# Raw float32 for the shared expert and router, a new plan of expert units, and gates between head pairs

## The chip, the cores and the metric

One core of a Trainium2 chip runs the kernel. The metric is the time of one execution in device microseconds. A matrix engine (TensorE, PE in the rows; PEld are its weight loads), VectorE (DVE), ScalarE (ACT), GpSimd (POOL) and SyncE (SP, which here only issues DMAs) have their own instruction streams and wait for one another by semaphores.

## The reference, cut to what matters

Two transformer blocks on 256 tokens of width 1024, all in float32.

The first block projects the normed input `h` to eight parts, runs a windowed attention (8 heads, with a bias table and a mask) and a grouped attention (8 query heads, 2 key heads, with norms and rotary positions), and merges them under two gates:

```python
proj = h @ w_in
qa, ka, va, qb, kb, vb, ga, gb = split(proj)
ya = neighbourhood_attention(qa, ka, va, rpb)
yb = gqa_attention(axial_rope(rmsnorm(qb)), axial_rope(rmsnorm(kb)), vb)
x = x + (sigmoid(ga) * (ya @ w_proj_a) + sigmoid(gb) * (yb @ w_proj_b)) @ w_out
```

A large layer of retrieved experts follows, and then the second block: a modulated mixer of two recurrences, and a mixture of 64 experts of which each token takes 8, with one shared expert:

```python
scores = sigmoid(h @ w_router)                  # 256 tokens x 64 experts
sel = scores + router_bias                      # 4 of 8 groups, then the 8 best experts
gates = chosen scores, normed, times 2.5
routed = sum over experts of (silu(h @ w_gate[e]) * (h @ w_up[e]) * gate[:, e]) @ w_down[e]
shared = (silu(h @ ws_gate) * (h @ ws_up)) @ ws_down
```

## The kernel before, in words

**Split products.** Most weights come as blocks of 128 x 1024 float32 into a raw tile; `split` (lines 66, 67) has ACT copy it to a high half `whi` in the faster matmul format float32r and DVE (or POOL, where asked) subtract to get the low half `wlo`. `mm3` (lines 80 to 82) multiplies high by high, high by low and low by high. `wide_load` makes a loader over a ring of raw tiles, and another over pairs of halves; with `whole` it returns the raw tile unsplit, which is multiplied in float32.

**First block** (`block1_mix`). The normed input is turned to `hT` (high and low). `stationary` and `moving` multiply it by the blocks of `w_in`, with 4 raw tiles and 2 pairs of halves. The program's order is: queries and keys of the windowed attention, its values, the four head pairs of the windowed attention, the projections of the grouped one, their norms and rotation on DVE (lines 270 to 309), its four head pairs, and the 16 gate blocks (lines 314 to 319), the first eight of which have POOL subtract. The mask is added to the bias table by one POOL instruction over 3072 elements (line 246). Only the first DMAs have an order written out by hand; for the rest a planner orders each engine's instructions, so gates and projections may run under an attention.

**Mixture** (`moe`). From the last steps of the mixer on, SP, PE, DVE and ACT keep the order of the program. The shared expert's four gate/up blocks and the router's block are split; its two down blocks are raw (`shared_up`, line 1587; the router, lines 1603 to 1605; `shared_down`). Then comes the choice of experts, a chain of small DVE steps (lines 1637 to 1774), which sorts the experts by their count of tokens into ranks and gives SP the list `lst` of their addresses. The first `STATIC` experts are put at the front whatever their count, so that their weights can be asked for before the list (`pre`).

The ranks are put into units of 128 columns of tokens: ranks below `WIDE` have all 128, below `MID` 96, below `LIGHT` 64, below `REST` 32. `mixture` joins them: a 96 with a 32, two of 64, four of 32 (or two of 32 and one of 64), and orders the kinds by a place between 0 and 1. Columns that a rank doesn't have are run by extra branches, which are taken only if a count is larger. An expert's weights are four gate/up blocks and two down blocks, and TensorE works on narrow columns of several experts side by side.

`run` goes through the units. In the turn of unit u TensorE does the gate/up matmuls (line 1559), between them the gather of a later group of two units (line 1743) and the turn of the unit before (line 1570), then the combining of unit u - 2 into the four sums in PSUM (line 1840) and the down matmuls of unit u - 1 (line 1578). `ahead` asks for weights on SP in the order of their use; a ring of 25 tiles takes them: raw tiles of the stage (4), of a pool opened at the start of `moe` (4) and of a later one (3), two tiles of the modulation, and the tiles of the shared weights' halves (12).

Of the kernel before, what the change touches and what calls it, by code (L numbers as in the profile page):

```python
# [19 lines left out]
P = 128  # L20
# [33 lines left out]
def uid(e, s):  # L54
    e.n += 1
    return f"{s}_{e.n}"
# [86 lines left out]
def block1_mix(e, a, x, begin):  # L143
# [22 lines left out]
    qkT = pool.tile([P, 8, T], F32, name="qkT")  # L166

    def stationary(blk, out, eng=None):
# [10 lines left out]
    def moving(blks, width, per):  # L179

        pt = [ps.tile([P, 512], F32, tag="mm", name=uid(e, "pmv"), bufs=e.mm_bufs) for _ in range(2)]
        for i, b in enumerate(blks):
            wh, wl = load_w(e, a["w_in_b"][b])
# [56 lines left out]
    for b in (0, 4, 1, 5):  # L240
# [5 lines left out]
    nc.gpsimd.tensor_tensor(bias.rearrange("p a b c -> p (a b) c"), bias.rearrange("p a b c -> p (a b) c"),  # L246
                            mask[:, None, :].to_broadcast([P, 48, 64]), op=OP.add)
# [9 lines left out]
    bv = bias.rearrange("p h v c -> p h (v c)")  # L257
# [22 lines left out]
    for tt, qk in enumerate(qks):  # L280
# [28 lines left out]
        nc.vector.tensor_copy(kT[:, :, tt * P:(tt + 1) * P], p[:, :2])  # L309
    for pair in range(4):  # L310
# [4 lines left out]
    sg = keep.tile([P, 16, T], F32, name="sg")  # L315
    for b in range(16):
        p = ps.tile([P, 512], F32, tag="mm", name=uid(e, "pg"), bufs=e.mm_bufs)
        stationary(8 + b, p[:, :T], nc.gpsimd if b < 8 else None)
        nc.scalar.activation(sg[:, b], p[:, :T], AF.Copy)
# [1076 lines left out]
STATIC = 2  # L1396
WIDE = 7
MID = 16
LIGHT = 30
REST = 50  # L1400
AHEAD = 8
RAW0 = 4
RAW1 = 3
# [41 lines left out]
def mixture():  # L1445

    few = iter(range(LIGHT, REST))
    kinds = [[shared((r, P)) for r in range(STATIC, WIDE)],
             [shared((r, 96), (next(few), 32)) for r in range(WIDE, MID)],
             [shared((r, 64), (r + 1, 64)) for r in range(MID, LIGHT, 2)]]  # L1450
    few = list(few)
    kinds.append([shared(*((r, 32) for r in few[i:i + 4])) for i in (0, 4)] + [shared((few[8], 32), (few[9], 32), (few[10], 64))])
    at = lambda k, j, n: j / (n - 1) if k == 0 else (j + 0.5) / n
    order = sorted((at(k, j, len(us)), k, u) for k, us in enumerate(kinds) for j, u in enumerate(us))
    return [u for _, _, u in order]
# [12 lines left out]
def moe(e, a, x, m, late, out):  # L1468
# [6 lines left out]
    load = wide_load(e, [(early, RAW0), (e.stage, e.raw_bufs)], [(early, 4), (e.stage, e.w_bufs)])  # L1475
# [28 lines left out]
    wg = [load(a["ws_gu"][b]) for b in range(2)]  # L1504
# [8 lines left out]
    wg.append(load(a["ws_gu"][2]))  # L1513
    wr = load(a["w_router"], eng=nc.gpsimd)
# [8 lines left out]
    hT = pool.tile([P, 2, NC8, T], F32R, tag="ehT", name="ehT")  # L1523
    hT = [hT[:, i] for i in range(2)]
# [4 lines left out]
    lows = [turned(e, h[0], 4 * n, 0, *hT) for n in range(2)]  # L1529
    add_to(1, m.po[1], 1, mod[2])  # L1530
    square(1, 1)
    for f in lows:
        f()
# [13 lines left out]
    def gu_block(pg, xh, xl, b, w):  # L1547
        for k in range(2):
            c = 2 * b + k
            s = slice(k * 512, (k + 1) * 512)  # L1550
            for j, (l, r) in enumerate(((xh, 0), (xh, 1), (xl, 0))):
                nc.tensor.matmul(pg, l[:, c], w[r][:, s], start=c == 0 and j == 0, stop=c == NC8 - 1 and j == 2)
# [34 lines left out]
    def shared_up(tt, b):  # L1587
        gu_block(pg[tt], hT[0][:, :, tts[tt]], hT[1][:, :, tts[tt]], b, wg[b])
# [5 lines left out]
    wg.append(load(a["ws_gu"][3], eng=nc.gpsimd))  # L1594
    lows = [turned(e, h[1], 4 * n, 1, *hT) for n in range(2)]
    for f in lows:
        f()
# [4 lines left out]
    wh, wl = (w.rearrange("p (c n) -> p c n", c=NC8) for w in wr)  # L1602
# [17 lines left out]
    wd = [load(a["ws_dn"][k], True) for k in range(2)]  # L1620
    units = [[(r, 0, P, 0)] for r in range(STATIC)] + mixture()
# [5 lines left out]

    load.raw[:0] = [(early, 4, t) for _ in range(4) for t in ("whi", "wlo")]
    load.raw[:0] = [(e.stage, e.w_bufs, t) for _ in range(e.w_bufs) for t in ("whi", "wlo")]
# [174 lines left out]
    def run(units, acc=(), new=None, ready=()):  # L1804
# [39 lines left out]
        ahead(1)  # L1844
# [63 lines left out]
        v = pool.tile([P, NC8, 2, T], F32R, tag="ehT", name=uid(e, "v")).bitcast(F32)  # L1908
        for tt in range(2):
            half = [slice(n * 512, (n + 1) * 512) for n in range(2)]  # L1910
            vs = [v[:, 2 * tt + n].rearrange("p a b -> p (a b)") for n in range(2)]
# [24 lines left out]
    if e.overflow:  # L1936
        with tc.If(nc.values_load(moreu[:, 5:6], min_val=0, max_val=T) > 0):
# [5 lines left out]
            with tc.If(v[2] > 0):  # L1943
                run([shared((r, 64), (r + 1, 64), base=64) for r in range(MID, LIGHT, 2)] + [shared((MID, P), base=P)])
            with tc.If(v[1] > 0):
                run([shared((r, P), base=96) for r in range(WIDE, MID)]
                    + [shared(*((r, 32) for r in range(WIDE, WIDE + 4)), base=224)])
# [97 lines left out]
```

## Time and profile before

| | |
|---|---|
| median of 3 runs | 1759.52 us (1758.49 to 1759.73) |
| the profiled execution | 1763.74 us, its span 1761.9 us |
| busy share: PE, DVE, ACT, POOL | 94%, 64%, 43%, 11% |
| DMA | 390.91 MB, mean 222 GB/s |
| mean granted clock of TensorE | 0.981 of full speed |

All rows are of the profiled execution, with times from its span's start. A share of busy time is a mean over stages that have different limits; windows and waits tell them apart. The first block runs until about 176 us, the layer of retrieved experts until about 1050, the mixer until about 1285, and the mixture from there to the end.

### The profile page before, as it was taken

What the parts mean: (1) busy time and instruction counts of PE and PEld (TensorE: products, weight loads), DVE (VectorE), ACT (ScalarE), POOL (GpSimd) and SP (SyncE); (2) the same over time, 40 slices, a digit from 0 to 9 for tenths busy, and PEclk for the clock granted to TensorE, in tenths of its full rate; (3) what the DMA queues carried; (4) which work ended last, traced back from release to release, by engine and by line L of the source; (5) the groups of instructions that cost most, each with busy time, mean ns of one, the idle gap of its engine ahead of it and who ended that gap; (6) DMA issues with size and microseconds to landing.
All of it is one profiled execution on the core that took longest, in us unless ns stands there. A gap on an engine that the chain in (4) does not pass through costs nothing.

```text
span 1761.9 us, 29814 instructions
## 1 busy us (share of the span) xinstructions
PE 1660.2 (94%) x11419; PEld 1307.8 (74%) x11419; DVE 1133.1 (64%) x2214; ACT 750.5 (43%) x1224; POOL 190.5 (11%) x95
## 2 busy tenths in 40 slices
PE   6989999899989999999999997987989999999996
PEld 6778888899989999777788776977875444444443
DVE  5675779995989999877777767688673111111112
ACT  3547544444544444444444455655552222222222
POOL 1030001222111222000000003023020000000000
PEclk9999999999999999999999999998999999999999
DMA  6423654556545555587888754532067799999993
GB/s 232 131 84 109 214 163 158 160 158 192 155 126 162 169 171 177 172 283 265 308 283 295 261 165 144 181 118 72 13 238 282 266 392 409 409 402 409 409 409 132
DMA packets 108118, 390.91 MB, mean 222 GB/s; under 512 B 12656, under 2 KB 12944, under 8 KB 107840
## 3 DMA queue, kind: packets, MB, share of 16 engines
q1 hardware_dynamic: 106128, 384.58, 62.7%
q0 software_dynamic: 976, 2.82, 0.5%
q8 instruction: 91, 1.49, 0.3%
q10 hardware_dynamic: 864, 1.53, 0.3%
q14 instruction: 59, 0.48, 0.1%
HBM read 386.79 MB, written 2.10 MB: 221 GB/s over the span
## 4 chain that ended last, share of the span: by engine, by line
PE 67%; DVE 18%; DMA 7%; issue 4%; ACT 3%; POOL 0%; SPq 0%; DVEq 0%; ACTq 0%
PE pgu L1559 11%; PE acc L686 10%; PE py L1578 6%; PE pu L80 5%; PE pu L81 5%; PE pu L82 5%; DVE wlo L67 5%; DMA raw<-in_w_ada 4%; PE pga L1743 3%; PE py L1840 3%; PE pg L632 2%; ACT whi L66 2%; PE pmv L81 1%; PE pmv L82 1%; PE pmv L80 1%
## 5 line engine op out<-in xcount | busy, mean ns | idle before, releaser
L66 ACT ACTIVATE whi<-raw 128x1024 fp32r<-128x1024 f32 x366 | 384.5, 1054 | 307.7 <-PE pu L81 136.7
L67 DVE TENSOR_TENSOR wlo<-raw,whi 128x1024 fp32r<-128x1024 f32 x310 | 383.4, 1239 | 83.1 <-ACT whi L66 82.0
L82 PE MATMUL pu<-pxT,wlo 128*128 128x256 f32 x1024 | 289.7, 283 | 9.2 <-DVE wlo L67 6.7
L80 PE MATMUL pu<-pxT,whi 128*128 128x256 f32 x1024 | 292.3, 285 | 0.8 <-ACT whi L66 0.8
L81 PE MATMUL pu<-pxT,whi 128*128 128x256 f32 x1024 | 288.9, 282 | 0.0
L686 PE MATMUL acc<-whi,hh 128*128 128x512 f32 x1008 | 280.7, 396 | 8.5 <-ACT hh L66 5.8
L686 PEld LDWEIGHTS acc<-whi,hh 128*128 128x128 f32 x1008 | 189.1, 189 | 53.9 <-ACT hh L66 6.8
L67 POOL TENSOR_TENSOR wlo<-raw,whi 128x1024 fp32r<-128x1024 f32 x56 | 149.6, 2675 | 661.9 <-ACT whi L66 607.2
L82 PEld LDWEIGHTS pu<-pxT,wlo 128*128 128x128 f32 x1024 | 195.3, 191 | 11.1 <-DVE wlo L67 8.1
L80 PEld LDWEIGHTS pu<-pxT,whi 128*128 128x128 f32 x1024 | 195.4, 191 | 1.0 <-ACT whi L66 1.0
L81 PEld LDWEIGHTS pu<-pxT,whi 128*128 128x128 f32 x1024 | 195.4, 191 | 0.0
L1559 PE MATMUL pgu<-raw,xg 128*32 128x512 f32 (+2 forms) x1012 | 193.8, 597 | 0.0
L686 PE MATMUL acc<-wlo,hh 128*128 128x512 f32 x504 | 157.5, 393 | 2.8 <-DVE wlo L67 2.8
L66 ACT ACTIVATE hh<-H 128x256 fp32r<-128x256 f32 x126 | 52.6, 417 | 174.6 <-PE acc L686 169.9
L1559 PEld LDWEIGHTS pgu<-raw,xg 128*32 128x32 f32 (+2 forms) x1012 | 55.6, 124 | 92.3 <-issue 82.1
L686 PEld LDWEIGHTS acc<-wlo,hh 128*128 128x128 f32 x504 | 95.0, 189 | 24.3 <-DVE wlo L67 4.2
L67 DVE TENSOR_TENSOR yl<-py,yh 128x512 fp32r<-128x512 f32 x52 | 36.0, 691 | 110.7 <-ACT yh L66 110.6
L1578 PE MATMUL py<-raw,th 128*32 128x512 f32 (+2 forms) x504 | 99.9, 599 | 0.5 <-ACT th L1572 0.5
L1564 DVE SCALAR_TENSOR_TENSOR hh<-hh,sv,pgu 128x256 f32<-128x256 f32 x26 | 12.4, 478 | 124.5 <-ACT hh L1563 124.5
L771 DVE SCALAR_TENSOR_TENSOR ada<-raw,cs,ada 128x1024 f32<-128x1024 f32 x48 | 61.5, 1282 | 40.6 <-DMA raw<-in_w_ada 40.6
L1746 ACT ACTIVATE xg<-pga 128x256 f32<-128x256 f32 x104 | 40.0, 384 | 111.6 <-PE pga L1743 107.6
L1743 PEld LDWEIGHTS pga<-S,hs 128*128 128x128 f32 x416 | 54.5, 188 | 36.8 <-issue 36.1
(567 smaller groups left out, 2919.5 us busy)
## 6 DMA issues: line engine op xcount, KB each, us to landing
raw<-in_w_gu SPq DMA_DIRECT2D x186, 512.0 KB, 9.6
raw<-in_peer_u SPq DMA_DIRECT2D x128, 512.0 KB, 3.6
raw<-in_peer_v SPq DMA_DIRECT2D x128, 512.0 KB, 4.5
raw<-in_w_dn SPq DMA_DIRECT2D x90, 512.0 KB, 10.1
raw<-in_w_ada SPq DMA_DIRECT2D x48, 512.0 KB, 4.8
raw<-in_w_in_a SPq DMA_DIRECT2D x24, 512.0 KB, 3.6
raw<-in_w2a SPq DMA_DIRECT2D x17, 512.0 KB, 4.4
raw<-in_w_out SPq DMA_DIRECT2D x16, 512.0 KB, 3.6
```

What stands on the lines that cost most here:

```text
L66: e.nc.scalar.activation(hi, src, AF.Copy)
L67: (eng or e.nc.vector).tensor_sub(lo, src, hi.bitcast(F32))
L80: nc.tensor.matmul(out, lh, rh, start=first, stop=False)
L81: nc.tensor.matmul(out, lh, rl, start=False, stop=False)
L82: nc.tensor.matmul(out, ll, rh, start=False, stop=last)
L686: nc.tensor.matmul(acc[tt][n], h[l][:, s], w[r][:, n * 512:(n + 1) * 512], start=j == order[0] and i == 0, stop=j == order[-1] and i == 2)
L771: nc.vector.scalar_tensor_tensor(mod[n], w, cs[:, c:c + 1], mod[n], op0=OP.mult, op1=OP.add)
L1559: nc.tensor.matmul(pg[t], xx[:, c, t], ws[i][:, k * 512:(k + 1) * 512], start=c == 0, stop=c == NC8 - 1)
L1578: nc.tensor.matmul(py[q][t], th[:, k, t], w[i][:, q * 512:(q + 1) * 512], start=k == 0, stop=last and k == 1)
L1743: nc.tensor.matmul(p[:, :n].rearrange("p u n -> p (u n)"), hs[i][:, tt, q * P:(q + 1) * P], S[:, tt, :n].rearrange("p u n -> p (u n)"), st ...
L1746: nc.scalar.activation(xg[:, q, :n], p[:, :n], AF.Copy)
L1840: nc.tensor.matmul(acc[tt][n], St[:, tt * P:(tt + 1) * P], y[:, n * 512:(n + 1) * 512], start=first and v == 0 and w == 0, stop=v == len(u ...
```

## The change: what it does

1. `moe`: the shared expert and the router multiply raw float32 tiles, in one matmul each; the turned input is kept once, not as two halves. The pool at the start has 12 raw tiles in place of 4 and 8 halves, the later one 5 in place of 3.
2. Three fixed experts in place of two; `WIDE` 6 for 7, `MID` 14 for 16. The list has 25 units, not 26: 3 fixed, then 3 of one expert, 8 of 96 + 32, 8 of 64 + 64 and 3 of four times 32, one of which is the first after the fixed.
3. `ahead` counts blocks of both kinds, up to 27, the size of the ring now.
4. `block1_mix`: `w_in` uses 4 pairs of halves; the windowed attention stands behind the grouped projections and their rotation; two gates stand behind each head pair of both attentions, all split by ACT and DVE; the mask is added by DVE, two heads at a time.

```diff
     def stationary(blk, out, eng=None):
-        wh, wl = load_w(e, a["w_in_a"][blk], eng=eng)
+        wh, wl = load(a["w_in_a"][blk], eng=eng)
...
-    nc.gpsimd.tensor_tensor(bias.rearrange("p a b c -> p (a b) c"), bias.rearrange("p a b c -> p (a b) c"),
-                            mask[:, None, :].to_broadcast([P, 48, 64]), op=OP.add)
...
-    for pair in range(4):
-        attention(pair, lambda q: qkT[:, q], lambda q: qkT[:, 4 + q],
-                  lambda q, kc: va[:, kc, q * P:(q + 1) * P], lambda h: bv[:, h], yT[0])
...
+    def gate(b):
+        p = ps.tile([P, 512], F32, tag="mm", name=uid(e, "pg"), bufs=e.mm_bufs)
+        stationary(8 + b, p[:, :T])
+        nc.scalar.activation(sg[:, b], p[:, :T], AF.Copy)
...
+    def masked(h):
+        if h % 2 == 0:
+            v = bias[:, h:h + 2].rearrange("p a b c -> p (a b) c")
+            nc.vector.tensor_tensor(v, v, mask[:, None, :].to_broadcast([P, 12, 64]), op=OP.add)
+        return bv[:, h]
+
+    for pair in range(4):
+        attention(pair, lambda q: qkT[:, q], lambda q: qkT[:, 4 + q],
+                  lambda q, kc: va[:, kc, q * P:(q + 1) * P], masked, yT[0])
+        for b in (2 * pair, 2 * pair + 1):
+            gate(b)
     for pair in range(4):
         attention(pair, lambda q: qT[:, q], lambda q: kT[:, q // 2],
                   lambda q, kc: vb[:, kc, q // 2].rearrange("p a b -> p (a b)"), None, yT[1])
-    for b in range(16):
...
+        for b in (8 + 2 * pair, 9 + 2 * pair):
+            gate(b)
...
-STATIC = 2
-WIDE = 7
-MID = 16
+STATIC = 3
+WIDE = 6
+MID = 14
...
-AHEAD = 8
-RAW0 = 4
-RAW1 = 3
+LEAD = 27
+RAW0 = 12
+RAW1 = 5
...
+    kinds = [[shared((r, P)) for r in range(STATIC, WIDE)],
+             [shared((WIDE + i, 96), (few[i], 32)) for i in range(n)],
+             [shared((r, 64), (r + 1, 64)) for r in range(MID, LIGHT, 2)],
+             [shared(*((r, 32) for r in few[i:i + 4])) for i in range(n, len(few), 4)]]
+
+    at = ([0.15, 0.33, 0.84], None, None, [0.0, 0.3, 0.8])
...
-            for j, (l, r) in enumerate(((xh, 0), (xh, 1), (xl, 0))):
-                nc.tensor.matmul(pg, l[:, c], w[r][:, s], start=c == 0 and j == 0, stop=c == NC8 - 1 and j == 2)
+            nc.tensor.matmul(pg, x[:, c], w[:, k * 512:(k + 1) * 512], start=c == 0, stop=c == NC8 - 1)
...
-        mm3(e, p[:, :T], wh[:, c], wl[:, c], hT[0][:, c], hT[1][:, c], c == 0, c == NC8 - 1)
+        nc.tensor.matmul(p[:, :T], wr[:, c], hT[:, c], start=c == 0, stop=c == NC8 - 1)
...
-        def ahead(n=AHEAD):
-            while len(ready) < len(order) and sum(1 - o[0] for o in order[taken[0]:len(ready)]) < n:
+        def ahead(n=LEAD):
+            while len(ready) < min(len(order), taken[0] + n):
```

The extra branches are cut anew to the same effect, and the loads of the shared weights and the router lose their splits.

## Rows read from the trace of the kernel before

**Rows 1.** The page's first part: busy us (share of the span) xinstructions of each engine.
```profile
PE 1660.2 (94%) x11419; PEld 1307.8 (74%) x11419; DVE 1133.1 (64%) x2214; ACT 750.5 (43%) x1224; POOL 190.5 (11%) x95
```

**Rows 2.** Windows by stage: stretch, length, busy us (xinstructions) per engine, clock, DMA, GB/s.
```profile
15.00:30.00 15.00, 11.55 (x79) 11.34 (x79) 8.62 (x7) 3.22 (x4) 6.78 (x1) 0.89 0.51 168
...
90.00:130.00 40.00, 31.58 (x213) 29.02 (x211) 30.77 (x58) 19.42 (x39) 17.30 (x7) 0.91 0.26 79
130.00:176.00 46.00, 45.55 (x316) 40.35 (x315) 24.78 (x48) 32.32 (x64) 0.00 (x0) 1.00 0.37 115
1285.00:1312.00 27.00, 23.36 (x105) 17.84 (x103) 21.47 (x32) 12.63 (x21) 4.10 (x5) 1.00 0.89 332
...
1385.50:1708.40 322.90, 322.70 (x2188) 145.66 (x2188) 52.64 (x120) 69.94 (x165) 0.00 (x0) 1.00 1.01 398
```

**Rows 3.** Chain of waits in the experts' stretch: start us, us, what.
```profile
1380.27 1.88 PE py L1840 x8
...
1385.59 3.57 PE pgu L1559 x32
...
1708.42 1.88 PE py L1840 x8
...
1734.17 1.89 PE py L1840 x8
...
1742.55 3.45 PE py L1578 x8
```

**Rows 4.** Windows, and SP's waits (total us, times, longest), experts' stretch.
```profile
1365.00:1425.00 60.00, 59.96 (x375) 28.50 (x377) 10.23 (x23) 13.56 (x32) 0.00 (x0) 1.00 0.83 290
1425.00:1720.00 295.00, 294.82 (x2006) 132.65 (x2002) 47.40 (x107) 63.64 (x150) 0.00 (x0) 1.00 1.03 408
...
1730.00:1746.00 16.00, 15.39 (x71) 7.30 (x69) 2.07 (x4) 2.95 (x6) 0.00 (x0) 1.00 0.02 6
...
SPq L1417 <- PE pgu L1559: 31.6, 37, 2.7
SPq L1811 <- DVE lst L1765: 14.4, 1, 14.4
```

**Rows 5.** Chain of waits, then groups by line (busy, mean ns, idle before), shared expert.
```profile
1323.13 5.81 PE pgu L1552 x24
...
1348.27 3.43 PE pgu L1559 x8
...
L81 PE MATMUL po<-wlo,mhT 128*128 128x512 f32 x29 | 11.4, 393 | 1.1 <-DVE wlo L67 1.1
L1552 PE MATMUL pgu<-whi,ehT 128*128 128x512 f32 x32 | 10.8, 404 | 0.7 <-DVE ehT L1344 0.7
...
L1341 PE MATMUL ptr<-ident,eh 128*128 128x128 f32 x16 | 2.3, 277 | 1.6 <-DVE eh L1496 0.8 <-PE po L82 0.8
```

**Rows 6.** Timeline, start of the first block: start us, us, engine, line, operation.
```profile
16.90 6.78 POOL L246 TENSOR_TENSOR bias<-bias,mask 128x3072 f32<-128x3072 f32 x1 [15.58 <-DMA mask<-in_na_mask]
...
19.38 5.38 DVE L67 TENSOR_TENSOR wlo<-raw,whi 128x1024 fp32r<-128x1024 f32 x1 [0.55 <-ACT whi L66]
...
24.82 0.38 PE L82 MATMUL pqk<-hT,wlo 128*128 128x256 f32 x1 [3.45 <-DVE wlo L67]
25.02 1.21 DVE L67 TENSOR_TENSOR wlo<-raw,whi 128x1024 fp32r<-128x1024 f32 x1
```

**Rows 7.** Timeline of DVE, and POOL's splits grouped by line, first block.
```profile
107.01 2.88 DVE L283 TENSOR_TENSOR qk<-qk,gq 128x512 f32<-128x512 f32 x1
...
111.16 0.68 DVE L299 TENSOR_TENSOR qk<-qk,ro 128x512 f32<-128x512 f32 x1
...
L67 POOL TENSOR_TENSOR wlo<-raw,whi 128x1024 fp32r<-128x1024 f32 x8 | 19.7, 2458 | 85.9 <-ACT whi L66 83.9 <-PE pg L82 2.0
```

**Rows 8.** Chain of waits, second attention, first pair.
```profile
120.25 1.07 PE pS L204 x8
...
127.51 1.79 PE pY L235 x8
```

More of the change, by code (lines that the diff above doesn't have):

```diff
@@ L1445, in mixture @@
 def mixture():
-    few = iter(range(LIGHT, REST))
+    few = list(range(LIGHT, REST))
+    n = MID - WIDE
     kinds = [[shared((r, P)) for r in range(STATIC, WIDE)],
[L1449 to L1454, printed above, removed]
+             [shared((WIDE + i, 96), (few[i], 32)) for i in range(n)],
+             [shared((r, 64), (r + 1, 64)) for r in range(MID, LIGHT, 2)],
+             [shared(*((r, 32) for r in few[i:i + 4])) for i in range(n, len(few), 4)]]
+    at = ([0.15, 0.33, 0.84], None, None, [0.0, 0.3, 0.8])
+    order = sorted((at[k][j] if at[k] else (j + 0.5) / len(us), k, u) for k, us in enumerate(kinds) for j, u in enumerate(us))
     return [u for _, _, u in order]
@@ L1474, in moe @@
     mod = m.mod
-    load = wide_load(e, [(early, RAW0), (e.stage, e.raw_bufs)], [(early, 4), (e.stage, e.w_bufs)])
+    load = wide_load(e, [(early, RAW0), (e.stage, e.raw_bufs)], [])
     def add_to(t, p, n, g):
@@ L1503, in moe @@
     square(0, 0)
-    wg = [load(a["ws_gu"][b]) for b in range(2)]
+    wg = [load(a["ws_gu"][b], True) for b in range(2)]
     for i in range(4):
@@ L1522, in moe @@
     hs = [pool.tile([P, 2, D], F32R, name=f"hs{i}") for i in range(2)]
-    hT = pool.tile([P, 2, NC8, T], F32R, tag="ehT", name="ehT")
-    hT = [hT[:, i] for i in range(2)]
+    hT = pool.tile([P, NC8, T], F32, tag="ehT", name="ehT")
     load.raw.extend([(pool, RAW1, "raw")] * RAW1)
@@ L1528, in moe, with turn_in @@
         normed(0, r, n)
-    lows = [turned(e, h[0], 4 * n, 0, *hT) for n in range(2)]
+    def turn_in(tt, n):
+        p = ps.tile([P, 4, P], F32, tag="tr", name=uid(e, "ptr"), bufs=e.tr_bufs)
+        for k in range(4):
+            nc.tensor.transpose(p[:, k], h[tt][:, (4 * n + k) * P:(4 * n + k + 1) * P], e.ident)
+        nc.scalar.activation(hT[:, 4 * n:4 * n + 4, tt * P:(tt + 1) * P], p, AF.Copy)
+    for n in range(2):
+        turn_in(0, n)
     add_to(1, m.po[1], 1, mod[2])
     square(1, 1)
-    for f in lows:
-        f()
     r = root(1)
@@ L1593, in moe @@
         normed(1, r, n)
[L1594 to L1597, printed above, removed]
+    wg.append(load(a["ws_gu"][3], True))
+    for n in range(2):
+        turn_in(1, n)
     load.raw.extend([(mod[k], None, None) for k in (2, 4)])
@@ L1620, in moe @@
     wd = [load(a["ws_dn"][k], True) for k in range(2)]
+    used = len(wg) + 1 + len(wd)
+    mine = [q for q in load.raw if q[0] is early]
+    load.raw[:] = (mine[used:] + [q for q in load.raw if q[0] is not early]
+                   + [(e.stage, e.w_bufs, t) for _ in range(e.w_bufs) for t in ("whi", "wlo")] + mine[:used])
     units = [[(r, 0, P, 0)] for r in range(STATIC)] + mixture()
@@ L1626, in moe @@
         pre.append(load((a["w_gu"], a["w_dn"])[which][(4, 2)[which] * r + b], True))
-    load.raw[:0] = [(early, 4, t) for _ in range(4) for t in ("whi", "wlo")]
-    load.raw[:0] = [(e.stage, e.w_bufs, t) for _ in range(e.w_bufs) for t in ("whi", "wlo")]
     hsh, psh = [], []
@@ L1843, in run @@
         new2 = None
-        ahead(1)
+        ahead()
         todo = []
@@ L1907, in run @@
         combine(len(units) - 1, *y)
-        v = pool.tile([P, NC8, 2, T], F32R, tag="ehT", name=uid(e, "v")).bitcast(F32)
+        v = pool.tile([P, NC8, T], F32, tag="ehT", name=uid(e, "v"))
         for tt in range(2):
             half = [slice(n * 512, (n + 1) * 512) for n in range(2)]
-            vs = [v[:, 2 * tt + n].rearrange("p a b -> p (a b)") for n in range(2)]
+            vs = [v[:, 4 * tt + 2 * n:4 * tt + 2 * n + 2].rearrange("p a b -> p (a b)") for n in range(2)]
             for n, s in enumerate(half):
@@ L1943, in moe @@
             with tc.If(v[2] > 0):
-                run([shared((r, 64), (r + 1, 64), base=64) for r in range(MID, LIGHT, 2)] + [shared((MID, P), base=P)])
+                run([shared((r, 64), (r + 1, 64), base=64) for r in range(MID, LIGHT, 2)]
+                    + [shared((r, 64), (r + 1, 64), base=P) for r in (MID, MID + 2)])
             with tc.If(v[1] > 0):
                 run([shared((r, P), base=96) for r in range(WIDE, MID)]
-                    + [shared(*((r, 32) for r in range(WIDE, WIDE + 4)), base=224)])
+                    + [shared(*((r, 32) for r in range(q, q + 4)), base=224) for q in (WIDE, WIDE + 4)])
             with tc.If(v[0] > 0):
```

21 lines of the change are left out of this document (9 added, 12 removed).

## The prediction

> **What bounds the kernel now.** The share of busy time comes first: TensorE works 94% of the span, so a gain must come from work it loses, from its idle time, or from time at the lower clock [rows 1]. The windows by stage say where each lies [rows 2]. From 1385.5 to 1708.4 us, the stretch in which the routed experts run, TensorE is busy 322.70 of 322.90 us. So the end is set there by how many units TensorE goes through. But the DMA engines are full in the same stretch, 408 GB/s from 1425 to 1720 us [rows 4]: a unit less of TensorE work helps only if the weights come early enough. In the first block TensorE has gaps in two places, 15 to 30 and 90 to 130 us, and its granted clock is below full there, 0.89 and 0.91, which is a mean of its two levels, 2.4 and 1.2 GHz [rows 2]. From 1285 to 1312 us (start of the shared expert) it idles 3.6 us more.
>
> **Change 1: the plan of units, 26 to 25.** Before, from the third unit on, the list has 5 units of one expert, 9 of 96+32 columns, 7 of 64+64 and 3 with three or four experts, behind 2 fixed units; after, 3, 8, 8 and 3 behind 3 fixed. In both there are 19 units with more than one expert, so just one unit of one expert goes (7 to 6). What is a unit worth? The chain of waits shows its combining step (L1840) once per unit. From 1380.27 to 1708.42 us there are 21 steps, 15.63 us each; the two from 1708.42 to 1734.17 take 12.9 each, because no later unit is gathered for beside them [rows 3]. The list of 25 still has 21 units past the first two beside which a later group is gathered, and then one in place of two without. So it is a short unit that goes: 12.9 us, not 15.6. The last group then holds one unit, and the gather for it, beside two units, is half as wide. The trace has no gather of that width: all that a later group costs beside a unit is 15.63 - 12.9 = 2.7 us, so half of it at two units is at most 2.7 saved, and at worst the narrow matmuls take as long as the wide ones and nothing is saved (I know no reason for more). I take 0, as the instructions stay as many. The term is -12.9 us, ends -15.6 and -12.9.
>
> The columns must hold the tokens, or the extra branches run. I counted the experts' tokens by evaluating the reference on its inputs: experts 0 to 2 get 69, 2 and 103, the others in order 107, 96, 89, 89, 88, 86, 81, ... with 74 as the last at 96 columns, 60 the first at 64, 33 the last at 64, 31 the first at 32, and the 51st 0. All fit, before and after.
>
> **Change 2: the weights ahead.** 50 experts have 6 blocks of 128 x 1024 float32, 0.524 MB; at 408 GB/s one takes 1.285 us and all 300 take 385.5 us, against 21 x 15.63 + 2 x 12.9 = 354 us for the units from 1380.27 to 1734.17 and three more around them. Today 10 blocks are asked for before the router's list is known, then SP waits 14.4 us for that list [rows 4], and from 1365 to 1425 us the rate is 290 GB/s, which loses 60 x (1 - 290/408) = 17.4 us: SP waits for TensorE to give buffers back (31.6 us on the gate/up matmuls alone) [rows 4]. After, 16 blocks go out before the list, since the shared weights are not split and the 8 tiles of halves serve as buffers. The ring has 27 places in place of 25. Three fixed units still use up only 6 blocks each, so the ring is full until the four-expert unit starts; I put it at 1385.5 us, where the fourth unit starts today [rows 3]. By then 16 used + 27 = 43 blocks are there. The 257 others need 330 us: the last lands near 1716. The last down blocks are used 12.9 us before today's 1742.55 [rows 3], at 1729.6, so 13 us are spare. The tightest place is behind the third four-expert unit (unit 19): block 254, its last down block, lands at 1385.5 + 211 x 1.285 = 1656.6, and is used about 10 us into the turn of unit 20 at 1385.5 + 17 x 15.63 = 1651.2: 5 us spare. Hence TensorE stays the bound, and I cost this edit at 0, with 5 us on the upper side if that cover is gone (10 GB/s less over those 211 blocks are 6.8 us).
>
> The Trainium skill speaks against this: SBUF — State Buffer, "Summary: rules for kernel authors", has about 358 GB/s for transfers between HBM and SBUF. By that figure the 157 MB would take 439 us and no unit less could show. The trace moves 408 GB/s for 295 us on end [rows 4], so I go by the row.
>
> **Change 3: shared expert and router on raw float32.** A float32 matmul is two records of 0.43 us in the trace (8 in 3.43 us), three split products are three of 0.242 (24 in 5.81 us) [rows 5]. Per block of two chunks that is 4 x 0.43 = 1.72 against 6 x 0.242 = 1.45, so 8 blocks add 2.2 us; the router's 8 matmuls 256 wide, 16 records of half of 0.43, are 3.4 us against 24 x 0.121 = 2.9, 0.5 more. What goes: five splits of weights on ACT, three on DVE, two on POOL, and the four low halves of the turned input. TensorE's waits on such are 1.1 us (half of an output weight, whose split stands behind two shared ones), 0.7 on a low half, 1.6 on the normed rows, which come late on DVE behind splits [rows 5]; I take all 3.4 as gone. Behind the router stands a chain of small DVE steps which starts earlier, but it is held by TensorE's shared work too, now longer. Sum: +2.7 - 3.4, about -0.7 us; ends -4 (the waits go, the added matmuls hide in the later gaps of that chain) and +2.7 (none goes).
>
> **Change 4: the first block.** (a) POOL's addition of the mask (6.78 us from 16.90) leaves; a DVE split beside it takes 5.38 us where the next takes 1.21, and TensorE waits 3.45 us for it [rows 6]; the clock of 0.89 over 15 us [rows 2] costs at most 1.65 us, nearly all with TensorE working. Without it 3.45 + 1.6 = 5 us go. DVE adds the mask in four pieces of 768 elements, an estimated 768/512 x 0.68 = 1.0 us each by the row of 512 elements [rows 7], before the attention and not among the first splits. (b) Eight gate splits leave POOL, 2.46 us each, and become DVE splits of 1.2 us, 10 us in all; beside POOL's, a rope step of 512 elements takes 2.88 us where the same width takes 0.68 [rows 7]. TensorE loses 8.4 us of idle time from 90 to 130 and, at 0.91 of the clock, up to 0.09 x 40 = 3.6 more [rows 2]. But the rope steps (two dozen on DVE, an estimated 16 us at 0.68 per 512 elements) now stand ahead of the windowed attention in the program; what TensorE has under them is the gates, and their splits queue behind rope on DVE. Four pairs of weight tiles in place of two let three gates be split before, 3 x 24 x 0.12 = 8.6 us of cover. (c) Under windowed attention TensorE had ten projection blocks as filler and has now two gates per pair (5.8 us); that is what kept it busy beside the other attention, 45.55 of 46 us from 130 to 176 [rows 2]. No row shows the new order, and the order of the engines' work is not written out by hand here. Bounds for (b) and (c): -12 (all idle time and clock loss goes) and +8 (rope's 16 us bare, less the three gates, with nothing won). I take -4. Term: -9 us, ends -17 and +3.
>
> **Sum.** -12.9 + 0 - 0.7 - 9 = -22.6 us. The profiled execution took 1763.74 us (span 1761.9); it would be 1741.1. The three runs' median is 1759.52, 4.2 less, so I predict 1737.
>
> **Rivals.**
> 1. The weights become the bound. For: DMA is already full for 295 us, and today's last block has landed by 1730 [rows 4], some 13 us before its use. Against: the 17.4 us lost around 1400 lie before the stretch in which it would matter. If the ring gives nothing, the end of the transfers stays near 1729 and the units save about 2 us: 1759.5 - 2 - 9.7 = 1748.
> 2. All idle time of the first block goes: 1759.5 - 12.9 - 0.7 - 17 = 1729. For: gates wait for nothing but their weights. Against: DVE is the engine that fills 90 to 130 us (30.77 of 40) and gets more to do.
> 3. Slower: the attention's chain lies bare. One pair's scores to its output take 7.3 us (120.25 to 127.51) [rows 8], and if program order binds TensorE so that two gates cover it badly, each of 8 pairs loses up to that much. From 3 us a pair the 22.6 us are spent; at 4 us a pair and nothing won in (b), it is 1759.5 - 18.6 + 32 = 1773. Against it: the same chain is covered today by gates in the same engine's queue.
> 4. The change doesn't do what it says: counts on the chip differ from mine and an extra branch runs, 8 or more units of 12.9 us, over 1830. Against: the columns for those ranks leave room, and the zero at rank 51 is as needed before.
>
> **Chances.** Forecast 0.66, rival 1 0.13, rival 2 0.14, rival 3 0.06, rival 4 0.01. The range reaches from rival 2's side to rival 1: 1724 to 1750. A measurement of this kernel tells 0.2% (3.5 us) from no change; slower takes rivals 3 and 4, 0.05 of their 0.07 (part of rival 3 ends near nothing), same 0.04, faster 0.91.
>
> **What would show it.** In the changed trace: 25 combining steps, the last pitch near 12.9, TensorE's idle time from 1385 on still under 1 us; if it waits there for DMA of expert weights, rival 1. At 15 to 30 us no split over 1.3 us on DVE and no wait of 3.5; between 90 and 130 us idle time about half of 8.4, and no slow rope step. If TensorE's idle time in the first block grows past 20 us, rival 3. The prediction is wrong if the units save less than 8 us or the first block gets longer.

## The result, and the profile after

The changed kernel takes 1735.95 us (median of 4 runs, 1730.54 to 1741.7), the kernel before 1759.62 beside it: a ratio of 0.9863, 95% interval 0.9828 to 0.9897. That is 23.7 us less; forecast were 22.6 less and 1737. One of the six executions of e9_two_pairs below ran at a granted clock of 0.748 and took 2050.76 us: its ratio leaves it out, and the median of the other five is 1738.43.

The first part of the page of the kernel after answers to [rows 1]: TensorE has 118 records fewer and 16.3 us less busy time, POOL 28.3 us less.

```profile
PE 1643.9 (95%) x11301; PEld 1292.7 (75%) x11301; DVE 1117.3 (65%) x2212; ACT 745.1 (43%) x1217; POOL 162.2 (9%) x84
```

The windows of the kernel after, for [rows 2]. The mixture begins earlier here, so the shared expert's window stands at 1262 and the experts' at 1361.

```profile
15.00:30.00 15.00, 15.00 (x115) 14.99 (x115) 12.17 (x16) 5.33 (x6) 0.00 (x0) 1.00 0.61 214
90.00:130.00 40.00, 40.00 (x259) 33.22 (x258) 25.99 (x54) 30.19 (x60) 0.00 (x0) 1.00 0.42 133
130.00:176.00 46.00, 44.98 (x295) 38.20 (x294) 28.51 (x62) 28.73 (x65) 0.00 (x0) 1.00 0.24 70
1262.00:1287.00 25.00, 23.89 (x109) 18.80 (x108) 16.41 (x31) 10.27 (x20) 0.00 (x0) 1.00 0.80 313
1361.00:1700.00 339.00, 338.71 (x2238) 151.65 (x2236) 53.96 (x120) 71.96 (x171) 0.00 (x0) 1.00 1.01 401
```

In both gaps of the first block TensorE has no idle time left, and the granted clock is 1.00 where it was 0.89 and 0.91. What it waits for from 10 to 185 us (total us, times, longest) is little; before, the waits for `qk`, `wlo` and `S` alone were 4.1, 3.5 and 3.3 us.

```profile
PE ptr L126 <- DVE hT L130: 2.6, 1, 2.6
PE pqT L298 <- DVE qk L293: 1.7, 2, 1.2
PE pp L80 <- ACT yTb L66: 0.9, 1, 0.9
PE pg L82 <- DVE wlo L67: 0.2, 1, 0.2
```

In the experts' stretch one view differs from what was forecast. The chain of waits of the kernel after, combining steps and what stands between them:

```profile
1608.61 1.87 PE py L1854 x8
1624.69 2.07 PE py L1854 x8
...
1638.99 10.09 DMA ada<-in_w_gu
...
1657.84 2.06 PE py L1854 x8
1672.49 1.92 PE py L1854 x8
```

From 1624.69 to 1657.84 are two steps, 15.48 and 17.67 us by the records: a transfer of weights stands in the chain, in the turn behind the third four-expert unit. The same kind of turn behind the second one takes 16.14 us, so 1.5 are lost. The timeline of TensorE's weight loads there shows where. The last number of each row, in brackets, is the idle time before it (2.66 us in sum; loads that wait for nothing stand some 0.29 apart there, so not all of it is loss):

```profile
1645.87 0.19 PEld L1572 LDWEIGHTS pgu<-raw,xg 128*64 128x64 f32 x2 [0.84 <-DMA raw<-in_w_gu]
1646.56 0.62 PEld L1572 LDWEIGHTS pgu<-raw,xg 128*64 128x64 f32 x5 [0.50 <-DMA raw<-in_w_gu]
1647.84 0.19 PEld L1572 LDWEIGHTS pgu<-raw,xg 128*64 128x64 f32 x2 [0.23 <-DMA raw<-in_w_gu]
1649.12 0.13 PEld L1572 LDWEIGHTS pgu<-ada,xg 128*64 128x64 f32 x1 [1.09 <-DMA ada<-in_w_gu]
```

Two marks in each trace show where the time went: the first matmul of the retrieved experts' layer (the first block and what follows from its end lie ahead of it), and the stretch from the first to the last gate/up matmul of the routed experts. What lies between the marks is the retrieved experts, the mixer and the shared expert. All ratios are to the kernel before on the same chip. Each mark is from one traced execution.

| run | ratio, 95% interval | layer of retrieved experts starts | between | routed experts |
|---|---|---|---|---|
| before | 1 | 281.3 | 1066.8 | 385.5 |
| after | 0.9863 (0.9828 to 0.9897) | 267.1 | 1058.7 | 374.2 |
| e1_again | 0.9869 (0.985 to 0.9888) | 266.0 | 1065.2 | 374.7 |
| e2_first_block | 0.9933 (0.992 to 0.9946) | 265.7 | 1062.3 | 385.5 |
| e3_mixture | 0.9912 (0.9898 to 0.9927) | 280.4 | 1059.9 | 374.4 |
| e4_old_plan | 0.9914 (0.9895 to 0.9933) | 267.6 | 1063.1 | 385.5 |
| e5_mask_pool | 0.9846 (0.9829 to 0.9863) | 266.1 | 1064.8 | 374.6 |
| e6_gates_pool | 0.9908 (0.9889 to 0.9927) | 275.4 | 1059.7 | 374.8 |
| e7_old_order | 0.9842 (0.9818 to 0.9866) | 264.1 | 1055.8 | 374.2 |
| e8_single_early | 0.985 (0.983 to 0.987) | 267.0 | 1061.2 | 371.9 |
| e9_two_pairs | 0.9891 (0.9865 to 0.9917) | 274.6 | 1052.3 | 373.6 |
| e10_two_pairs_mask | 0.9932 (0.9913 to 0.9951) | 278.5 | 1059.8 | 374.3 |
| e11_order_single | 0.9813 (0.9794 to 0.9832) | 262.1 | 1062.2 | 371.9 |
| e12_ring19 | 0.9931 (0.9913 to 0.9949) | 266.8 | 1055.3 | 384.3 |

The stretch between varies from 1052 to 1067 us and follows no edit; it makes the total times of one kernel scatter by several us. The marks repeat far better: the six traces with the changed first block as it is (after, e1, e2, e4, e8, e12) have 265.7 to 267.6, 266.7 in the mean, and the experts of the eight with the changed mixture as it is (after, e1, e3, e5, e6, e7, e9, e10) take 373.6 to 374.8, 374.4 in the mean. The first block of before was traced twice, 281.3 and 280.4 (e3). So the verdicts below go by the marks, and the ratios stand beside them.

### The profile page after: what moved, and what is told of

Its sections match the earlier page's. It is cut to its first block, busy times and chain, and to the rows that moved or that the text cites. A ratio compares the mean times of both kernels' runs of the same rounds, so it can differ in the third digit from the quotient of the medians.

```text
span 1728.7 us, 29531 instructions
## 1 busy us (share of the span) xinstructions
PE 1643.9 (95%) x11301; PEld 1292.7 (75%) x11301; DVE 1117.3 (65%) x2212; ACT 745.1 (43%) x1217; POOL 162.2 (9%) x84
## 4 chain that ended last, share of the span: by engine, by line
PE 67%; DVE 17%; DMA 9%; issue 4%; ACT 3%; POOL 0%; DVEq 0%; SPq 0%; ACTq 0%
PE pgu L1572 10%; PE acc L696 8%; DMA raw<-in_w_ada 7%; PE py L1591 5%; PE pu L80 5%; PE pu L81 5%; PE pu L82 5%; DVE wlo L67 4%; PE pga L1757 3%; PE py L1854 3%; PE pg L642 2%; PE pmv L82 1%; PE pmv L80 1%; ACT whi L66 1%; PE pmv L81 1%
## 5 line engine op out<-in xcount | busy, mean ns | idle before, releaser
L66 ACT ACTIVATE whi<-raw 128x1024 fp32r<-128x1024 f32 x361 | 379.5, 1054 | 299.0 <-PE pu L81 138.5
L1572 PE MATMUL pgu<-raw,xg 128*32 128x512 f32 (+2 forms) x988 | 183.4, 597 | 0.0
L67 POOL TENSOR_TENSOR wlo<-raw,whi 128x1024 fp32r<-128x1024 f32 x46 | 128.1, 2788 | 499.6 <-ACT whi L66 498.1
L696 PEld LDWEIGHTS acc<-wlo,hh 128*128 128x128 f32 x504 | 94.8, 189 | 23.7 <-DVE wlo L67 3.8
L1591 PE MATMUL py<-raw,th 128*32 128x512 f32 (+2 forms) x508 | 93.7, 596 | 0.5 <-ACT th L1585 0.5
L1760 ACT ACTIVATE xg<-pga 128x256 f32<-128x256 f32 (+1 forms) x104 | 39.1, 376 | 110.7 <-PE pga L1757 106.6
```

The lines of the kernel that those rows point to most:

```text
L66: e.nc.scalar.activation(hi, src, AF.Copy)
L67: (eng or e.nc.vector).tensor_sub(lo, src, hi.bitcast(F32))
L696: nc.tensor.matmul(acc[tt][n], h[l][:, s], w[r][:, n * 512:(n + 1) * 512], start=j == order[0] and i == 0, stop=j == order[-1] and i == 2)
L1572: nc.tensor.matmul(pg[t], xx[:, c, t], ws[i][:, k * 512:(k + 1) * 512], start=c == 0, stop=c == NC8 - 1)
L1591: nc.tensor.matmul(py[q][t], th[:, k, t], w[i][:, q * 512:(q + 1) * 512], start=k == 0, stop=last and k == 1)
L1760: nc.scalar.activation(xg[:, q, :n], p[:, :n], AF.Copy)
```

## The experiments

**e1_again**: the changed kernel once more, for comparison on the same chip.

> The changed kernel once more, to see what of its profiled span is chance. Its execution on record was 33.2 us shorter in span than the one of before, while the medians are 23.7 apart: 14 us lie before the retrieved experts' first up matmuls, some 5 us between 703 and 1282 us, where nothing was changed, 3 at the shared expert, 11.3 in the units. Theory A: the 5 us in the unchanged stages are chance; a new profile has the first block 13 to 15 us shorter and the units 11 to 13, and a span of 1733 to 1740. Rival B: they follow from the change (another alignment of transfers), and then they show again, span 1727 to 1731.

1735.23 us, with a span of 1734.6: theory A, as the span says and the stretch between the marks, which is about as long as before again (1065.2 us). The first block is 15.3 us shorter and the experts 10.8, each just outside the theory's range. The long step is 18.34 us here, 17.91 in e3_mixture: the wait for weights is no accident of one run.

**e2_first_block**: the kernel before with only the first block's part of the change. **e3_mixture**: the opposite half, the changed mixture with the first block of before.

```diff
+    load = wide_load(e, [(e.stage, e.raw_bufs)], [(e.stage, e.w_bufs), (pool, 2)])
...
-        wh, wl = load_w(e, a["w_in_a"][blk], eng=eng)
+        wh, wl = load(a["w_in_a"][blk], eng=eng)
...
```

The cut shown is of e2. With the mask, the order and the gates' splits, e2 has the whole fourth point of the change, and nothing of the others.

> Only the first block is changed; the mixture is as before. Theory A (the terms add up): 13 to 15 us faster, about 1745.5, and the windows of the first block as in the changed kernel. My blind term was 9. Rival B: some of the gain is given back in the later stages, whose transfers start at other times, and less than 8 us is left.

> Only the mixture is changed (raw float32, ring of 27, 25 units); the first block is as before. Theory A: 11.3 in the units and 3 at the shared expert and router, about 14 us faster, 1745. Blind terms: 12.9 + 0.7. Rival: less than 9, if part of the 3 us was another alignment.

1746.3 and 1743.42 against 1757.34: -11.0 and -13.9, in sum -24.9, against -22.1 for both in e1_again. The halves add up within their intervals. e3 gives what its theory said. In e2 the time falls by less than the 13 to 15 us of its theory, though by the marks the first block gives 15.6 us there (0.9 in e3, where it is as before). So its rival B, that some of the gain is given back later, is not excluded; 4.6 us are also no more than the scatter between the marks. The experts give nothing in e2 and 11.1 in e3.

**e4_old_plan**: the changed kernel with the old 26 units, two fixed experts, and the new ring of 27.

```diff
-STATIC = 3
-WIDE = 6
-MID = 14
+STATIC = 2
+WIDE = 7
+MID = 16
```

> The changed kernel with the old plan of 26 units (two fixed experts, the old mixture of kinds); raw float32, the ring and the first block as in the change. Theory A: TensorE's count of units sets the end, so it is 11 to 13 us slower than the changed kernel, about 1748. Rival: the ring is what gave the gain behind 1326 us, and the old plan is within 4 us of the changed kernel.

1743.93, 8.7 us over e1_again, less than the 11 to 13 of the theory and clear of the rival's 4. The routed experts take 385.5 us, 11.1 more than with the new plan and exactly as before with the ring of 25: the ring by itself gives nothing while the plan is the old one.

**e5_mask_pool**: POOL adds the mask, as before.

```diff
+    nc.gpsimd.tensor_tensor(bias.rearrange("p a b c -> p (a b) c"), bias.rearrange("p a b c -> p (a b) c"),
+                            mask[:, None, :].to_broadcast([P, 48, 64]), op=OP.add)
```

> The changed kernel, with the mask added once by POOL up front as before the change, instead of by DVE in four pieces; nothing else is put back. Theory (the mask accounts for the waits at the start, 3.5 us and the low clock of 15 to 30 us, and the excess of the first block over its term lies with the gates): about 5 us slower than the changed kernel, lost before 30 us: a DVE split of 4 to 6 us beside POOL, a wait of TensorE of 3 us or more, the end of the first block's output projection near 188 us instead of 183. Rival 1 (the mask is most of the gain of 14 us): 10 us or more slower, projection near 193. Rival 2 (the wait was filled from other work): within 1.5 us of the changed kernel.

Rival 2 came true: the mark stands at 266.1, no later than the changed kernel's. The timelines of POOL, ACT and DVE at the start show why; the last two rows, for comparison, are DVE's in the kernel after:

```profile
16.90 7.92 POOL L247 TENSOR_TENSOR bias<-bias,mask 128x3072 f32<-128x3072 f32 x1 [15.58 <-DMA mask<-in_na_mask]
...
19.66 1.06 ACT L66 ACTIVATE whi<-raw 128x1024 fp32r<-128x1024 f32 x1 [3.60 <-DMA raw<-in_w_in_a]
...
15.76 2.35 DVE L67 TENSOR_TENSOR wlo<-raw,whi 128x1024 fp32r<-128x1024 f32 x2
...
21.65 0.42 DVE L178 COPY qkT<-pqk 128x256 f32<-128x256 f32 x1 [2.33 <-PE pqk L82]
24.41 0.42 DVE L178 COPY qkT<-pqk 128x256 f32<-128x256 f32 x1 [2.34 <-PE pqk L82]
24.75 2.35 DVE L67 TENSOR_TENSOR wlo<-raw,whi 128x1024 fp32r<-128x1024 f32 x2
```

```profile
24.93 0.42 DVE L178 COPY qkT<-pqk 128x256 f32<-128x256 f32 x1 [0.60 <-PE pqk L82]
25.27 2.35 DVE L67 TENSOR_TENSOR wlo<-raw,whi 128x1024 fp32r<-128x1024 f32 x2
```

With four pairs of halves DVE has done two splits by 18.11 us, and no split is due while POOL works on. ACT has the next high half ready at 20.72, and DVE splits it only at 24.75, close to POOL's end at 24.82; but that split stands behind a copy that waits for TensorE, and in the kernel after, where POOL does nothing then, it comes just as late, at 25.27, behind the same copy. So these rows don't show a split that stands still beside POOL, though the expectation of e10 below says so; the kernel before shows one [rows 6], and e10 again. Copies out of PSUM (the memory of TensorE's results) go on beside POOL and take their usual 0.42. TensorE is busy 15.00 of the 15 us.

**e6_gates_pool**: the first eight gates split by POOL, as before.

```diff
-        stationary(8 + b, p[:, :T])
+        stationary(8 + b, p[:, :T], nc.gpsimd if b < 8 else None)
```

> The changed kernel with the first eight gates' weights split on POOL as before the change; mask and order as changed. Theory (the gates' place among the head pairs and DVE free of POOL give most of the first block's gain): 4 to 9 us slower than the changed kernel, with TensorE waiting for split weights between 90 and 165 us and DVE steps of 2 us or more beside POOL's splits of 2.46 us. Rival (the new order alone covers it, and the engine that splits is indifferent): within 2 us of the changed kernel.

1742.37, the mark at 275.4, 8.7 us behind the changed kernel's mean: the theory. Timelines of POOL and DVE, and then TensorE's longest wait from 10 to 185 us:

```profile
77.75 7.62 POOL L67 TENSOR_TENSOR wlo<-raw,whi 128x1024 fp32r<-128x1024 f32 x3 [3.78 <-ACT whi L66]
...
77.94 2.88 DVE L277 TENSOR_TENSOR qk<-qk,gq 128x512 f32<-128x512 f32 x1
80.74 2.43 DVE L278 TENSOR_TENSOR qk<-qk,gk 128x128 f32<-128x128 f32 x1
83.10 2.82 DVE L277 TENSOR_TENSOR qk<-qk,gq 128x512 f32<-128x512 f32 x1
```

```profile
PE pqT L298 <- DVE qk L293: 9.7, 1, 9.7
```

Three rope steps (the rotation of queries and keys) take 8.13 us beside three splits of POOL, where the kernel after has 0.68, 0.28 and 0.68 for the same steps. Even the one of 128 elements takes 2.43: the price is POOL's instruction, not DVE's. TensorE then waits 9.7 us for the rotated queries where it waited 1.7. I had put the waits on the gates' weights between 90 and 165 us; it was rope, from 78 to 88.

**e7_old_order**: windowed attention ahead of the grouped projections, all gates behind both attentions; the rest as changed.

```diff
+    for pair in range(4):
+        attention(pair, lambda q: qkT[:, q], lambda q: qkT[:, 4 + q],
+                  lambda q, kc: va[:, kc, q * P:(q + 1) * P], masked, yT[0])
     pq = moving(range(4, 8), 512, 2)
...
-        for b in (8 + 2 * pair, 9 + 2 * pair):
-            gate(b)
+    for b in range(16):
+        gate(b)
```

> The changed kernel with the first block's program order as before: windowed attention ahead of the projections for the second attention, all 16 gates behind both attentions. Mask in four pieces and all splits on DVE and ACT as changed. Theory (the order gives about a third of the gain, the engines the rest): 3 to 6 us slower than the changed kernel, with TensorE idle 3 to 6 us between 90 and 130 us. Rival 1 (the order is all of the gain behind 90 us): 8 to 10 us slower. Rival 2 (the order gives nothing, POOL's absence all): within 1.5 us.

None of the three: the old order is better by the mark, 264.1, 2.6 us ahead of the changed kernel's mean and 1.6 ahead of its earliest; in e11 below, with the old order too, it is 262.1. The time, 1729.58 us, is lower too, but within the intervals. First the windows of the kernel after for 30 to 90 and 130 to 165 us, then those of e7_old_order for 30 to 90, 90 to 130 and 130 to 165:

```profile
30.00:90.00 60.00, 58.07 (x389) 52.74 (x388) 42.52 (x76) 30.04 (x45) 0.00 (x0) 1.00 0.52 164
...
130.00:165.00 35.00, 33.98 (x203) 27.20 (x202) 18.77 (x50) 23.25 (x59) 0.00 (x0) 1.00 0.15 46
```

```profile
30.00:90.00 60.00, 59.95 (x340) 48.98 (x339) 42.75 (x79) 33.58 (x70) 0.00 (x0) 1.00 0.43 139
90.00:130.00 40.00, 39.47 (x294) 35.79 (x292) 31.77 (x70) 27.01 (x48) 0.00 (x0) 1.00 0.42 130
130.00:165.00 35.00, 34.79 (x249) 31.56 (x249) 17.60 (x35) 21.53 (x44) 0.00 (x0) 1.00 0.33 99
```

From 30 to 165 us the new order idles 1.93 + 0 + 1.02 = 2.95 us, the old one 0.05 + 0.53 + 0.21 = 0.79. The new order leaves rope without enough cover, as I had feared, but for less than 3 us and not 16: TensorE's waits for rotated queries are 1.7 us, in e7 0.4, and the wait of 0.9 for the attention's output (`yTb`) is not there in e7.

**e8_single_early**: the last one-expert unit ahead of the third four-expert unit.

```diff
-    at = ([0.15, 0.33, 0.84], None, None, [0.0, 0.3, 0.8])
+    at = ([0.15, 0.33, 0.78], None, None, [0.0, 0.3, 0.8])
```

> The changed kernel with the last one-expert unit (of the plan's list) put ahead of the third four-expert unit, not three places behind it; the same 25 units. Theory (the 2 to 3 us in the unit behind the third four-expert unit are a wait for weights in a tight place, and there is room later): the long step of 17.7 to 18.3 us falls to about 15.6, TensorE's wait there goes, no new one comes, and the time is 1.5 to 3 us shorter. Rival (it is the sum of the transfers that binds): the wait comes back in the last four units, their steps are 2 to 3 us longer in sum, and the time stays the same.

The theory: the experts take 371.9 us, 2.5 less, and the long step is gone. Combining steps from its chain, for those of the kernel after above:

```profile
1626.22 2.06 PE py L1854 x8
1641.79 1.87 PE py L1854 x8
1657.42 2.06 PE py L1854 x8
1672.78 1.93 PE py L1854 x8
```

15.57, 15.63 and 15.36 us, and none of the later steps is longer than in the kernel after by more than 0.7. The wait was worth 1.5 to 2.2 (the long steps of 17.67, 17.91 and 18.34 against 16.14); the rest of the 2.5 goes with the new order of the units and isn't traced further. The ratio is 0.0019 below that of e1_again, 3.3 us, which the intervals alone could not have told from nothing.

**e9_two_pairs** takes the two further pairs of halves away; **e10_two_pairs_mask** has POOL add the mask on top of that.

```diff
-    load = wide_load(e, [(e.stage, e.raw_bufs)], [(e.stage, e.w_bufs), (pool, 2)])
+    load = wide_load(e, [(e.stage, e.raw_bufs)], [(e.stage, e.w_bufs)])
```

> The changed kernel without the two further pairs of tiles for split weights in the first block (two pairs, as before the change); mask, order and splitting engines as changed. Theory (the tiles are what lets splits run ahead of DVE's long stretches, and a good part of the first block's 14 us): 4 to 9 us slower than the changed kernel, with TensorE waiting for gates' split weights while DVE works on rope (66 to 90 us). Rival (the gain lies with POOL's absence, and two pairs are enough then): within 2 us.

> The changed kernel with two pairs of tiles for split weights (as in the run beside it) and the mask added by POOL up front as before the change. With four pairs the mask on POOL cost nothing, although a DVE split stood until POOL's 7.92 us were over. Theory (the further tiles hid that stall): 3 to 5 us slower than the run with two pairs and the mask on DVE, all of it before 30 us, with a wait of TensorE for wlo of about 3.5 us as in the kernel before. Rival (the stall before the change came from something else in the start): within 1.5 us of that run, no such wait.

1739.61 and 1745.16 us, and by the marks both theories. They are 274.6 and 278.5: 7.9 us for the two pairs, and 3.9 for the mask once they are gone. The longest wait in e9 is for rope's result, 4.6 us where it was 1.7; the gates' halves, to which I had put all of it, make 2.5. Waits of TensorE from 10 to 185 us, first e9, then e10, and e10's window at the start:

```profile
PE pqT L298 <- DVE qk L293: 4.6, 2, 2.3
...
PE pg L80 <- ACT whi L66: 1.6, 2, 0.8
PE pg L82 <- DVE wlo L67: 0.9, 1, 0.9
```

```profile
PE pqT L300 <- DVE qk L295: 4.7, 2, 2.4
PE pqk L82 <- DVE wlo L67: 3.3, 1, 3.3
```

```profile
15.00:30.00 15.00, 11.67 (x79) 11.44 (x79) 8.63 (x7) 3.28 (x4) 6.78 (x1) 0.89 0.49 166
```

The start of e10 is the start of before [rows 2, 6] again: a wait of 3.3 us for `wlo`, the clock at 0.89, POOL's 6.78.

**e11_order_single**: e7 and e8 together.

> The changed kernel with the first block's program order as before the change, and the last one-expert unit ahead of the third four-expert unit. Each alone took 3 us off its stretch (first block's end 180.0 in place of 183; the step of 17.7 to 18.3 us down to 15.7). Theory (two places that don't touch): both stretches as in the single runs, 4 to 6 us under the changed kernel, about 1730. Rival (an earlier end of the first block is given back on the way): within 2 us of the changed kernel.

1725.62 us (1722.62 to 1727.43), 0.9813 of before, the fastest of all: the mark at 262.1, the experts at 371.9. The two gains stand side by side, 4.6 and 2.5 us against the means of the changed kernel, and the theory's 4 to 6 was too little. The median is 9.6 us under e1_again's; what that is over the 7 is of the size of the scatter between the marks, where no edit was made. The interval lies below that of e1_again.

**e12_ring19**: 19 places in the ring of weights.

```diff
-LEAD = 27
-RAW1 = 5
+LEAD = 19
+RAW1 = 3
...
-                   + [(e.stage, e.w_bufs, t) for _ in range(e.w_bufs) for t in ("whi", "wlo")] + mine[:used])
+                   + mine[:used])
```

> The changed kernel with 19 places in the experts' ring of weights in place of 27 (no tiles of halves, two tiles fewer behind, lead 19); plan of 25 units as changed. Theory (the lead at the third four-expert unit is what the ring holds when it starts, and it is already short by 2 to 3 us): 8 blocks less at 1.28 us are 10 us less lead, so TensorE waits 8 to 13 us more for weights and the time is that much longer; the steps behind the second four-expert unit show waits too. Rival (the rate recovers, since only the sum of the transfers counts): within 3 us of the changed kernel.

1745.44 us; the experts take 384.3 us, 9.9 more: the theory. Steps of 20.74, 18.77 and 20.67 us by the records, where the kernel after has 16.14, 16.17 and 17.67, the first and the last behind a four-expert unit. Its windows, and its weight loads' waits for DMA:

```profile
1322.00:1380.00 58.00, 57.92 (x325) 30.18 (x325) 9.70 (x25) 12.76 (x32) 0.00 (x0) 1.00 0.76 264
1380.00:1700.00 320.00, 318.29 (x2049) 141.06 (x2049) 48.60 (x108) 66.68 (x160) 0.00 (x0) 1.00 1.03 408
```

```profile
PEld pgu L1572 <- DMA raw<-in_w_gu: 9.0, 14, 1.2
PEld py L1591 <- DMA raw<-in_w_dn: 5.6, 7, 1.1
```

In the kernel after the same two waits are 3.5 and 0.3 us from 1380 to 1700. From 1380 on the DMA runs at the same 408 GB/s. Before, less lands: 58 x 264 = 15.3 MB in the 58 us behind the first gate/up matmul, where the kernel after has 37 x 282 + 17 x 340 = 16.2 MB in 54 (its windows stand below). Counted from the landings in the traces, 33 of the experts' 300 blocks have come when the fourth unit starts, 41 in the kernel after: the 8 places fewer, 8 x 1.285 = 10.3 us of transfer against 9.9 lost.

## Why the prediction was right, and where not

The time was right, 1737 forecast and 1735.95 measured, and the units and the first block went the way that was forecast; but that it came within about a microsecond is luck. Two terms were off in opposite directions, the units by 1.8 us and the first block by 5.6, and together the marks give 2 to 4 us more (11.1 + 14.6 = 25.7) than the medians show (23.7 and, in e1, 22.1).

**Units: -12.9 forecast, -11.1 measured** (385.5 to 374.2, 374.7 and 374.4), short of the end of -12.9. The mechanism is the forecast one: 25 combining steps, one short step gone, the last full one 12.98 us. What is missing is the wait for weights: without it, and with the units in e8's order, it is -13.6, inside the ends. The gather of half the width, which I costed at nothing, saves about 1.1 us: by the records the two turns beside it take 14.56 and 15.17, where turns of the same kinds beside a full one take 14.73 and 16.11.

**The ring: 0 forecast with 5 us spare at the tightest place; a wait of 1.5 to 2.2 us came there.** The place was right within a unit, the spare not. Windows of the kernel after, from the fourth unit's start at 1363.38 on:

```profile
1326.00:1363.00 37.00, 36.94 (x168) 20.70 (x167) 5.03 (x14) 8.34 (x21) 0.00 (x0) 1.00 0.81 282
1363.00:1380.00 17.00, 16.99 (x123) 7.86 (x126) 3.83 (x10) 3.86 (x10) 0.00 (x0) 1.00 0.92 340
1380.00:1690.00 310.00, 309.72 (x2074) 139.72 (x2067) 48.75 (x109) 66.08 (x159) 0.00 (x0) 1.00 1.03 408
...
1690.00:1700.00 10.00, 10.00 (x42) 3.32 (x40) 1.38 (x2) 1.58 (x3) 0.00 (x0) 1.00 0.94 374
```

From 1363 to 1700 these are 17 x 340 + 310 x 408 + 10 x 374 GB/s = 136.0 MB, 259 blocks of 0.524 MB if all of it is experts' weights, so some 41 of the 300 had landed when the fourth unit began, where I had put 43: 2 x 1.285 = 2.6 us. The landings in the trace, counted, are 41. The 17 us at 340 in place of 408 lose 2.8 us more. Together 5.4 us, more than the whole spare of 5: I had let the full rate begin as soon as the ring was full. The loss that remains, some 0.4, is smaller than the wait; the rest is the estimate's own grain, a block or two.

What the ring is worth shows only with the new plan: nothing with 26 units (e4), 10 us with 25 (e12). Rival 1 had its price right: with a small ring the units would have saved 1.2 us (385.5 to 384.3; I had said about 2).

**Raw float32: -0.7 forecast.** From the mixer's last `pw` matmul (line 1174 before, 1184 after), ahead of its output projection, to the experts' first the traces take 72.6 us before and 71.0 in e2, which has the old mixture, and 70.4 and 71.4 after (after, e1): +0.4 to -2.2, a scatter larger than the term. The mechanism shows better: TensorE's idle time in that stretch falls from 7.4 to 3.8 us, so the waits went about as forecast (3.4), and its busy time grows from 65.2 (63.5 in e2) to 66.6 (67.6 in e1). The chain of the kernel after has the added work as worked out, 0.44 us for a record of 512 columns and 0.23 for one of 256:

```profile
1295.55 3.72 PE prt L1617 x16
...
1301.26 7.06 PE pgu L1565 x16
```

**First block: -9 forecast, -14.6 measured** (281.3 to 266.7), inside the ends of -17 and +3. The mis-sized term is (b) and (c), taken at -4. With (a) at its -5 they gave some -9.6. The waits and the lower clock of [rows 2] were 3.45 + 8.42 us of idle time and up to 1.65 + 3.6 of clock, 17.1 in sum; after, 2.95 of idle time are left and the clock is full, which makes 14.2. The windows from the start to the mark, before and after, agree: 9.6 us less idle time and 4.6 less busy time for nearly the same records.

```profile
0.00:281.30 281.30, 252.93 (x1689) 227.53 (x1689) 194.62 (x449) 145.93 (x274) 31.24 (x19) 0.97 0.48 155
```

```profile
0.00:267.10 267.10, 248.37 (x1687) 223.29 (x1688) 191.45 (x460) 148.10 (x276) 4.80 (x10) 0.99 0.51 163
```

Rival 2 names this outcome, and its objection, that DVE fills 90 to 130 us and gets more to do, failed: up to the mark DVE is busy 191.45 us in place of 194.62, with eight splits of 1.2 us and the mask's pieces more, and the stretched steps gone. The one slow row of 2.88 [rows 7] was to be read as one of a kind: from 104 to 118 us of the kernel before, DVE rows of 2.53, 2.88 and 2.70 stand beside POOL's splits, on the way to the rotated queries, where the kernel after has 0.89, 0.68 and 0.49.

The Trainium skill has a rule for such steps in SBUF — State Buffer, "Who interferes with whom": a VectorE instruction with two SBUF inputs and a GpSimd instruction that reads SBUF exclude each other, and whichever is issued first holds the shared ports to its end. The traces agree: DVE's step of 0.28 us takes 2.43 beside POOL splits of 2.54 each (e6), and copies out of PSUM are not held (e5).

By the parts: the mask's move, costed at -5, is worth 3.9 with two pairs of halves (e10 against e9) and nothing with four (e5), so it was not needed. The two pairs are worth 7.9 (e9), POOL's absence from the gates 8.7 (e6); these can't be added, as each was measured with the other in place: with only two pairs and the mask on POOL, the gates' move and the new order give 281.3 - 278.5 = 2.8 us together, where with four pairs they come to 8.7 - 2.6 = 6.1. So each seems to be worth more with the other. The two pairs on their own, with the gates on POOL in the old order, were not tried. The new order, from which I expected cover, costs 2.6 us (e7) to 4.6 (e11), and rival 3's mechanism (attention or rope bare under two gates) is real at that price, far below the 3 us a pair it needed.

**The signs named beforehand.** No DVE split over 1.3 us and no wait of 3.5 at the start: so. Idle time of 90 to 130 about half of 8.4: it is nothing, and no rope step is slow. 25 combining steps: so. TensorE's idle time from 1385 on under 1 us as the sign that the weights are in time: it is 0.29 of 339 us, and still the weights were late. That sign can't see the wait.

**Left open**: why the stretch between the marks takes 1052 us in one run and 1067 in another, and so whether it gives back part of the first block's gain. The sum of the terms rests on the profiled execution, and those of before and after differ by 33 us in span, 9.5 more than the medians; 8.1 us of the 33 lie there, of which up to 2 are the shared expert's.

## What to carry to other kernels

Count what a slow pass on a helper engine costs by the buffers behind it: the same POOL pass cost 3.9 us with two pairs of buffers, where a split of DVE fell into it, and nothing with four, where none was due. When the unit of work gets shorter, recount the tightest place of the weights' stream with the rate of its slow start, not only with the full one; then move a light unit ahead of the heavy one. And test a new order by itself: here, by the mark, it was the one part of the change that lost time.

## What the runs showed of the hardware

- A stall for weights can hide in busy time: in e12_ring19 the experts lose 9.9 us, and TensorE is busy 318.29 of 320 us. The waits stand at the weight loads (9.0 and 5.6 us, where the kernel after has 3.5 and 0.3) and in the distance of repeated steps; the busy share doesn't show them.
- POOL waits for DVE as DVE for POOL: the mask pass takes 7.92 us in e5, where DVE was at splits of 1.2 us when it began, and 6.78 in e10 and before, where it wasn't.
- DMA moved 408 GB/s for 310 us on end, again, with raw weights from a ring of 27 as with one of 19.
